# A two-layer encoder trunk: the first gate and up projections on unnormalised columns of x with the root of the norm applied later, and the matmuls of each bank sorted by width

## The chip, the cores and the metric

The kernel runs on one core of one Trainium2 chip. The metric is device time in microseconds (us) of one execution; the profile is one such execution on its own, and its times are read from the start of its span.

## The reference

Two layers, each a half-step SwiGLU feed-forward, a token mixing and a second half-step feed-forward. Every one of these six sub-layers normalises its input (root mean square, times a gain) and its output.

```
def rmsnorm(x, g):
    y = xf * lax.rsqrt(jnp.mean(xf * xf, axis=-1, keepdims=True) + NORM_EPS)
    return y * g
def swiglu(x, w_gate, w_up, w_down):
    return (jax.nn.silu(x @ w_gate) * (x @ w_up)) @ w_down
f = swiglu(rmsnorm(x, ffn1_pre_g[l]), ffn1_w_gate[l], ffn1_w_up[l], ffn1_w_down[l])
x = x + 0.5 * rmsnorm(f, ffn1_post_g[l])
```

x is 256 tokens by 1024 columns in float32, the gate and up weights are 1024 x 2816, the down weights 2816 x 1024. The root of the norm is one number per token, so it may be multiplied in before the projection, or after it on the projection's result. The token mixing (three groups of attention heads between one input and one output projection) is untouched by the change.

## The kernel before, in words

Precision is kept by splitting every float32 operand into a high part (rounded to the type that TensorE takes, fp32r) and the low remainder. A product then costs three products: high x high, high x low and low x high.

**Weights.** `Stream` takes all weights of both layers in one fixed list of chunks of 512 KB (for gate and up: 4 of the 8 rows of 128, times 256 columns). SP loads a chunk into one of 4 raw buffers (`load`, L116). `ahead(n)` cuts n half-chunks ("pieces"): ScalarE copies 128 x 512 into the high part `whi` (L139), VectorE subtracts to get the low part `wlo` (L140). After a chunk's second piece the next load is issued into the freed raw buffer. Nine chunks may be split ahead of the one in use (`NSPLIT`).

**Feed-forward, `ffn(i)`.** The activations lie in `xT`, columns on the partitions, 8 tiles, each with 256 tokens of high part beside 256 of low part. The first four of the 22 tiles of the hidden width (f = 0 to 3) go in token form (`gate`, `up`, `tokens_out`: tokens stationary, 256 weight columns moving, `mm3`, L373 to L375), one half of the tokens at a time, because the second half of the tokens is normalised later; their results are turned back by transposes (`token_close`, L507). The other 18 tiles (f = 4 to 20 in steps of two) go through `cols_pair`: two PSUM banks for gate and two for up per step. In a bank, for each of the 8 row tiles k, a wide matmul (128 x 512: high weights against high and low activations at once, L405) is followed by a narrow one (128 x 256: low weights against high activations, L407). After a bank ScalarE copies its low half out (L412), VectorE adds the halves (L413); after the second gate bank ScalarE takes silu (L552), after the second up bank VectorE multiplies (L558) and the product is split (L299, L300). Then `stream.ahead(6)` puts up to six pieces into the queues of ScalarE and VectorE. Four PSUM banks ("rot") turn in this loop. So VectorE's order in a step is fixed: two additions, pieces, two additions, product, split, pieces.

**Down, `down`.** 22 chunks of the down weights, 12 matmuls of 128 x 512 each, then post-norm, residual and the next pre-norm.

**The start.** x comes in rows (L185, L261), with the gain of the first norm broadcast to all partitions (L206) and the first four chunks behind it on SP's queue. `Norm.alone` squares x on ScalarE (L296), takes the root on GpSimd (L283), multiplies x by root and gain on VectorE (L345), TensorE transposes (L368) and ScalarE and VectorE split into `xT`. A hand-written list, `START`, places these steps between the pieces. 14 matmuls on `ident` keep TensorE at work before (L912). The gains of the next norms and the lambda vectors are loaded by GpSimd in the first feed-forward (L203, L198, L904).

Of the kernel before, what the change touches and what calls it, by code (L numbers as in the profile page):

```python
# [79 lines left out]


START = {
    "x1": 2,
    "warm": 14,
    "ops": [
        ["A0", "d", "p", "T00", "d", "T01", "p", "A1", "p"],
        ["d", "d"],
        ["d", "T10"],
        ["p", "T11"],
        ["d", "d", "d", "p", "d"],  # L90
    ],
}
WARM = START["warm"]
# [3 lines left out]
class Stream:  # L97
# [3 lines left out]
    def __init__(self, nc, raw_pool, split_pool):  # L101
        self.nc, self.raw_pool, self.split_pool = nc, raw_pool, split_pool
        self.src, self.raw, self.parts = [], {}, {}
        self.loaded = self.cut = self.used = self.piece = 0
        self.spare, self.in_spare = [], set()
# [4 lines left out]
    def load(self):  # L110
# [5 lines left out]
        self.nc.sync.dma_start(raw[:, : kt * n].rearrange("p (k n) -> p k n", n=n), ap)  # L116
        self.raw[i] = raw
        self.loaded += 1

    def ahead(self, pieces, lo=None):  # L120

        for _ in range(pieces):
            i = self.cut
            if i >= len(self.src):
                return
            if self.piece == 0:
                if i < self.used + NSPLIT + len(self.in_spare):
                    self.hi = self.split_pool.tile([P, CH], F32R, tag="whi", name=f"whi{i}")
# [10 lines left out]
            self.nc.scalar.copy(self.hi[:, a:b], raw[:, a:b])  # L139
            (lo or self.nc.vector).tensor_sub(self.lo[:, a:b], raw[:, a:b], self.hi.bitcast(F32)[:, a:b])  # L140
            self.piece += 1
            if self.piece == 2:
                self.parts[i] = (
                    self.hi[:, :m].rearrange("p (k n) -> p k n", n=n),
                    self.lo[:, :m].rearrange("p (k n) -> p k n", n=n),
                )
                self.raw.pop(i)
                self.cut, self.piece = i + 1, 0
                self.load()

    def get(self, i):
        return self.parts[i]
# [9 lines left out]
def trunk_kernel(  # L162
    ctx: ExitStack,
    tc: tile.TileContext,
    x, f1_pre, f1_gate, f1_up, f1_down, f1_post,
# [29 lines left out]
    def load_pre(i):  # L195
        if i < len(norms):
            pre_tiles[i] = work.tile([P, D], F32, tag="gpre", name=f"gpre{i}", bufs=1)
            nc.gpsimd.dma_start(pre_tiles[i], row_bcast(norms[i][0], norms[i][2], D))  # L198

    def load_post(i):  # L200
        if i < len(norms):
            post_tiles[i] = work.tile([P, D], F32, tag="gpost", name=f"gpost{i}", bufs=1)
            nc.gpsimd.dma_start(post_tiles[i], row_bcast(norms[i][1], norms[i][2], D))  # L203

    pre_tiles[0] = work.tile([P, D], F32, tag="gpre", name="gpre0", bufs=1)
    nc.sync.dma_start(pre_tiles[0], row_bcast(f1_pre, 0, D))  # L206
# [16 lines left out]
    def plan_ffn(gate, up, down, l):  # L223
        g = {}
        for key, ap, c0 in (("g", gate, 0), ("u", up, 0), ("g", gate, 1), ("u", up, 1)):
            for h in range(2):
                stream.add(rows(ap, l, 4 * h, 4 * h + 4, c0 * 256, c0 * 256 + 256), 4, 256)
        for f in range(4, KF, 2):
# [29 lines left out]

    for k in range(NRAW):
        if k == START["x1"]:  # L260
            nc.sync.dma_start(xs[:, 1, :], x_t[:, 1, :])  # L261
        stream.load()
# [5 lines left out]
    ones = work.tile([P, P], F32, tag="tc", bufs=3, name="ones")  # L268
# [33 lines left out]
    class Norm:  # L302
# [33 lines left out]
        def alone(self):  # L336

            t, nm = self.t, "pre" + self.nm
            ss = small.tile([P, 4], F32, tag="ss", name=f"sp_{nm}")
            self.xg = work.tile([P, D], F32, tag="xg", name=f"xg_{nm}", bufs=1)  # L340
            for h in range(2):
                mean_square(xs[:, t, HALVES[h]], ss, h, nm)
            r = rstd_of(halves_mean(ss, nm), 1, nm)
            for sl in HALVES:
                nc.vector.scalar_tensor_tensor(self.xg[:, sl], xs[:, t, sl], r[:, 0:1], pre_tiles[0][:, sl],  # L345
                                               ALU.mult, ALU.mult)

# [48 lines left out]
    def cols_pair(out, c, nm, between=lambda: None):  # L396

        for j in range(2):  # L400
            cs = slice(j * P, j * P + P)
            ps = psum.tile([P, 2, SEQ], F32, tag="rot", name=f"{nm}_{j}")
            for k in range(KT):
                wh, wl = stream.get(c + k // 4)
                nc.tensor.matmul(ps.rearrange("p a t -> p (a t)"), lhsT=wh[:, k % 4, cs],  # L405
                                 rhs=xT[:, k].rearrange("p a t c -> p (a t c)"), start=k == 0, stop=False)
                nc.tensor.matmul(ps[:, 1, :], lhsT=wl[:, k % 4, cs], rhs=xT[:, k, 0].rearrange("p t c -> p (t c)"),  # L407
                                 start=False, stop=k == KT - 1)
            if j == 0:
                between()  # L410
            side = work.tile([P, 512], F32, tag="tc", bufs=3, name=f"side_{nm}_{j}")[:, :SEQ]
            nc.scalar.copy(side, ps[:, 1, :])  # L412
            nc.vector.tensor_add(out[:, j, :], ps[:, 0, :], side)  # L413
# [53 lines left out]

    def ffn(i, turn1):
# [42 lines left out]
        sg00 = gate(0, 0, (lambda: start(1)) if i == 0 else None)  # L511
        if i == 0:
            start(2)
        h00 = up(sg00, 0, 0, (lambda: start(3)) if i == 0 else None)
        if i == 0:
            start(4)
        else:
            sg10 = gate(1, 0, turn1)
        sg01 = gate(0, 1)
        stream.done(2)  # L520
        if i == 0:
            stream.ahead(4)
        h01 = up(sg01, 0, 1)
        stream.done(2)
        stream.ahead(4)
        if i == 0:
            sg10 = gate(1, 0)
        sg11 = gate(1, 1)
        stream.done(2)
        stream.ahead(4)  # L530
        new_h()
        token_close(h00, 0, 0)
        h10 = up(sg10, 1, 0)
        token_close(h01, 0, 1)
        h11 = up(sg11, 1, 1)
        stream.done(2)
        stream.ahead(4)
        token_close(h10, 1, 0)
        load_pre(i + 1)
        if i % 3 == 0:  # L540
            load_lambda(i // 3)
        closing = [(h11, 1, 1)]
        for f in range(4, KF, 2):
            cc = stream.used

            def close():
                while closing:
                    token_close(*closing.pop())

            sg = work.tile([P, 512], F32, tag="ta", bufs=TA, name=f"sg{i}_{f}")  # L550
            cols_pair(sg.rearrange("p (a b) -> p a b", a=2), cc, f"pg{i}_{f}", close)
# [5 lines left out]
            cols_pair(hv, cc + 2, f"pu{i}_{f}")  # L557
# [3 lines left out]
            stream.ahead(6)  # L561
# [351 lines left out]
    first = [Norm(0, t) for t in range(2)]  # L913

    def start(n):
        for op in START["ops"][n]:
            if op == "d":
                stream.ahead(1)
            elif op == "p":
                stream.ahead(1, nc.gpsimd)  # L920
            elif op[0] == "A":
                first[int(op[1])].alone()
            else:
                first[int(op[1])].turn((int(op[2]),))

    start(0)
    load_post(0)
# [6 lines left out]
    "x", "ffn1_pre_g", "ffn1_w_gate", "ffn1_w_up", "ffn1_w_down", "ffn1_post_g",  # L934
# [32 lines left out]
```

## Time and profile before

| | us |
|---|---|
| three runs | 1020.24, 1024.27, 1023.5; median 1023.5 |
| the profiled execution, device time | 1022.65 |
| its span in the profile | 1020.7 |
| TensorE busy in the span | 996.7 (98%) |
| VectorE / ScalarE busy | 672.3 / 586.4 |
| first useful matmul | 11.59 |
| first wide matmul of the first feed-forward | 43.48 |
| first matmul of its down stage | 146.84 |

Between the device time and the span lie 1.95 us that no row shows. Instructions are pipelined, so the time of one row is longer than the step from its start to the next one's start; the steps are what adds up.

### The profile page before, as it was taken

How to read it: one execution, taken by the hardware profiler on the slowest of the kernel's cores; microseconds unless marked ns; L12 is line 12 of the kernel's file. 1: busy time of each engine (PE TensorE's matmuls, PEld its weight loads, DVE VectorE, ACT ScalarE, POOL GpSimd, SP SyncE). 2: the span in 40 equal slices, each digit the busy share in tenths (PEclk: the TensorE clock that was granted, in tenths of full speed). 3: DMA queues.
4: the chain of work that ended last, by engine and by line, in shares of the span. 5: the costliest groups of instructions: out<-in, count | busy, mean ns of one | idle time of the engine just before them, and what ended most of it. 6: DMA issues, size and time to landing. Idle time of an engine off the chain costs nothing.

```text
span 1020.7 us, 16031 instructions
## 1 busy us (share of the span) xinstructions
PE 996.7 (98%) x5940; PEld 874.6 (86%) x5940; DVE 672.3 (66%) x1345; ACT 586.4 (57%) x1265; POOL 43.2 (4%) x73
## 2 busy tenths in 40 slices
PE   8899999999999999999999999999989999999997
PEld 7788888899887988888899888888978789888886
DVE  4576675577686577765557767646678756866642
ACT  5465564466766566555446756545577655765531
POOL 3100000010000100000020000001000010000000
PEclk8999999999999999999999999999999999999999
DMA  8866656748344477656726865663853525765631
GB/s 265 234 201 181 196 171 228 199 131 235 101 145 124 145 219 217 185 201 210 223 69 206 249 197 173 227 192 118 253 150 105 158 90 175 240 202 189 215 114 41
DMA packets 151005, 183.16 MB, mean 179 GB/s; under 512 B 5744, under 2 KB 134896, under 8 KB 150928
## 3 DMA queue, kind: packets, MB, share of 16 engines
q1 hardware_dynamic: 148448, 174.08, 55.7%
q0 software_dynamic: 2192, 7.54, 2.5%
q8 instruction: 46, 0.75, 0.3%
q10 hardware_dynamic: 288, 0.52, 0.1%
q14 instruction: 31, 0.25, 0.1%
HBM read 181.08 MB, written 1.05 MB: 178 GB/s over the span
## 4 chain that ended last, share of the span: by engine, by line
PE 83%; DVE 5%; DMA 5%; ACT 4%; issue 1%; POOL 0%; SPq 0%; DVEq 0%; POOLq 0%; ACTq 0%
PE pg L405 13%; PE pu L405 13%; PE acc L373 9%; PE acc L375 9%; PE acc L374 9%; PE pg L407 7%; PE pu L407 7%; DVE wlo L140 3%; DMA raw<-in_w_in_dram 2%; PE pp L373 2%; DMA raw<-in_ffn_w_up_dram 2%; PE pp L375 2%; PE pp L374 1%; ACT p_b L722 1%; PE pu L374 1%
## 5 line engine op out<-in xcount | busy, mean ns | idle before, releaser
L140 DVE TENSOR_TENSOR wlo<-raw,whi 128x512 fp32r<-128x512 f32 (+1 forms) x625 | 395.6, 688 | 157.1 <-ACT whi L139 156.8
L139 ACT CAST whi<-raw 128x512 fp32r<-128x512 f32 x630 | 349.8, 617 | 122.0 <-PE acc L375 71.3
L405 PE MATMUL pg<-xT,whi 128*128 128x512 f32 x576 | 207.1, 401 | 0.0
L405 PE MATMUL pu<-xT,whi 128*128 128x512 f32 x576 | 205.2, 399 | 0.0
L407 PE MATMUL pg<-xT,wlo 128*128 128x256 f32 x576 | 162.3, 282 | 0.0
L407 PE MATMUL pu<-xT,wlo 128*128 128x256 f32 x576 | 161.8, 281 | 0.0
L373 PE MATMUL acc<-whi,hh 128*128 128x512 f32 x352 | 137.2, 390 | 0.0
L374 PE MATMUL acc<-wlo,hh 128*128 128x512 f32 x352 | 137.0, 389 | 0.0
L375 PE MATMUL acc<-whi,hl 128*128 128x512 f32 x352 | 137.0, 389 | 0.0
L405 PEld LDWEIGHTS pg<-xT,whi 128*128 128x128 f32 x576 | 108.9, 189 | 26.7
L405 PEld LDWEIGHTS pu<-xT,whi 128*128 128x128 f32 x576 | 108.2, 188 | 27.0
L407 PEld LDWEIGHTS pg<-xT,wlo 128*128 128x128 f32 x576 | 109.5, 190 | 0.0
L407 PEld LDWEIGHTS pu<-xT,wlo 128*128 128x128 f32 x576 | 108.8, 189 | 0.0
L375 PEld LDWEIGHTS acc<-whi,hl 128*128 128x128 f32 x352 | 66.1, 188 | 13.9
L373 PEld LDWEIGHTS acc<-whi,hh 128*128 128x128 f32 x352 | 66.1, 188 | 13.6
L374 PEld LDWEIGHTS acc<-wlo,hh 128*128 128x128 f32 x352 | 66.1, 188 | 13.4
L373 PE MATMUL pp<-xT,whi 128*128 128x256 f32 x256 | 76.4, 298 | 0.0
L374 PE MATMUL pp<-xT,whi 128*128 128x256 f32 x256 | 73.0, 285 | 0.0
L375 PE MATMUL pp<-xT,wlo 128*128 128x256 f32 x256 | 73.0, 285 | 0.0
L412 ACT COPY side_pu<-pu 128x256 f32<-128x256 f32 x72 | 26.1, 368 | 50.3 <-PE pu L407 50.3
L373 PEld LDWEIGHTS pp<-xT,whi 128*128 128x128 f32 x256 | 49.4, 193 | 4.9 <-issue 4.2
L413 DVE TENSOR_TENSOR h<-pu,side_pu 128x256 f32<-128x256 f32 x72 | 29.8, 422 | 30.4 <-ACT side_pu L412 30.2
(247 smaller groups left out, 1455.1 us busy)
## 6 DMA issues: line engine op xcount, KB each, us to landing
raw<-in_ffn_w_gate_dram SPq DMA_DIRECT2D x88, 512.0 KB, 4.8
raw<-in_ffn_w_up_dram SPq DMA_DIRECT2D x88, 512.0 KB, 4.6
raw<-in_ffn_w_down_dram SPq DMA_DIRECT2D x88, 512.0 KB, 4.4
raw<-in_w_in_dram SPq DMA_DIRECT2D x36, 512.0 KB, 5.3
raw<-in_w_out_dram SPq DMA_DIRECT2D x16, 512.0 KB, 3.5
raw<-in_w_in_dram SPq DMA_DIRECT2D x8, 576.0 KB, 4.3
gpost<-in_ffn_post_g_dram POOLq DMA_DIRECT2D x4, 512.0 KB, 4.3
raw<-in_w_in_dram SPq DMA_DIRECT2D x4, 384.0 KB, 3.4
```

The lines of the kernel that those rows point to most:

```text
L139: self.nc.scalar.copy(self.hi[:, a:b], raw[:, a:b])
L140: (lo or self.nc.vector).tensor_sub(self.lo[:, a:b], raw[:, a:b], self.hi.bitcast(F32)[:, a:b])
L373: nc.tensor.matmul(ps, lhsT=ah, rhs=bh, start=first, stop=False)
L374: nc.tensor.matmul(ps, lhsT=ah, rhs=bl, start=False, stop=False)
L375: nc.tensor.matmul(ps, lhsT=al, rhs=bh, start=False, stop=last)
L405: nc.tensor.matmul(ps.rearrange("p a t -> p (a t)"), lhsT=wh[:, k % 4, cs], rhs=xT[:, k].rearrange("p a t c -> p (a t c)"), start=k == 0, ...
L407: nc.tensor.matmul(ps[:, 1, :], lhsT=wl[:, k % 4, cs], rhs=xT[:, k, 0].rearrange("p t c -> p (t c)"), start=False, stop=k == KT - 1)
L412: nc.scalar.copy(side, ps[:, 1, :])
L413: nc.vector.tensor_add(out[:, j, :], ps[:, 0, :], side)
L722: nc.scalar.activation(p[:, a:b], p[:, a:b], AF.Exp, bias=st[:, t : t + 1], scale=-1.0, accum_out=st[:, 2 + t : 3 + t])
```

## The change

**The start.** The host lays x out a second time, in columns (`x_cols`, with the first gain as 8 columns ahead of it; a transposition, no arithmetic). SP loads it in four quarters of 256 KB, each followed by half a gate chunk. `prepare` multiplies columns by the gain while it splits them (ScalarE's copy with a scale, VectorE's multiply-subtract); the root is left out. f = 0 to 3 now go in column form too (`cols_pieces`: for each quarter of x, 6 narrow matmuls into each of two banks), for all 256 tokens at once, with no transposes. Squares are taken on ScalarE and summed on GpSimd while the first up projection runs; a matmul with ones sums over partitions, GpSimd takes the root, and a second matmul with a diagonal spreads it into `rb` (128 x 256). VectorE multiplies every gate and up result of the first feed-forward by `rb`: per bank for f = 0 to 3, per pair of banks (128 x 512) in the nine steps of the loop. `START` is gone, and so are the transposes of x; 10 matmuls on `ident` stand ahead instead of 14. The rows of x, needed for the residual, are loaded at f = 10 and f = 16, the first post gain, the second pre gain and the lambda vectors after f = 20, the gains on SP's queue instead of GpSimd's. `ahead` takes 4 pieces instead of 6 up to f = 4 of the first feed-forward.

**All four feed-forwards.** `cols_pair` issues the eight wide matmuls of a bank first and the eight narrow ones behind them. The first four tiles of the other three feed-forwards stay in token form.

```
+    def pass_hi(ps, c, k, cs):
+        wh = stream.get(c + k // 4, k % 4 // 2)[0]
+        nc.tensor.matmul(ps.rearrange("p a t -> p (a t)"), lhsT=wh[:, k % 4, cs],
+                         rhs=xT[:, k].rearrange("p a t c -> p (a t c)"), start=k == 0, stop=False)
...
             for k in range(KT):
-                wh, wl = stream.get(c + k // 4)
-                nc.tensor.matmul(ps.rearrange("p a t -> p (a t)"), lhsT=wh[:, k % 4, cs],
-                                 rhs=xT[:, k].rearrange("p a t c -> p (a t c)"), start=k == 0, stop=False)
-                nc.tensor.matmul(ps[:, 1, :], lhsT=wl[:, k % 4, cs], rhs=xT[:, k, 0].rearrange("p t c -> p (t c)"),
-                                 start=False, stop=k == KT - 1)
+                pass_hi(ps, c, k, cs)
+            for k in range(KT):
+                pass_lo(ps, c, k, cs)
...
+        def prepare(p):
+            for k in (2 * p, 2 * p + 1):
+                hi, lo = (xT[:, k, b].rearrange("p t c -> p (t c)") for b in range(2))
+                nc.scalar.activation(hi, xc[:, k, :], AF.Copy, scale=gcol[:, k : k + 1])
+                nc.vector.scalar_tensor_tensor(lo, xc[:, k, :], gcol[:, k : k + 1], hi.bitcast(F32),
+                                               ALU.mult, ALU.subtract)
+            stream.ahead(1)
+        def before_up(p):
+            for n in ((0, 1), (2,), (3,), ())[p]:
+                squares(n)
+            stream.ahead(1)
...
+        pg = cols_pieces(c, "pg0_0", prepare, lambda p: None, "acc")
+        pu = cols_pieces(c + 2, "pu0_0", before_up, after_up)
...
+                cols_pair(sv, cc, f"pg{i}_{f}", close)
+                if rb is not None:
+                    nc.vector.tensor_mul(sv, sv, rb.unsqueeze(1).broadcast_to([P, 2, SEQ]))
             nc.scalar.activation(sg, sg, AF.Silu)
             stream.done(2)
-            stream.ahead(6)
+            stream.ahead(4 if rb is not None and f < 6 else 6)
...
+            if i == 0 and f in (10, 16):
+                t = int(f == 16)
+                nc.sync.dma_start(xs[:, t, :], x_t[:, t, :])
+            if i == 0 and f == KF - 2:
+                load_post(0, nc.sync)
+                load_pre(1, nc.sync)
+                load_lambda(0)
```

How instructions stand on the engines, at three places. TensorE at the first banks of the loop, before; `pg0_4_0` is gate bank 0 of f = 4, `whi8` and `wlo8` the parts of its first chunk, `pth` a transpose of the token form:

```order
L405 MATMUL pg0_4_0_547<-xT_83,whi8_328 128x512
L407 MATMUL pg0_4_0_547<-xT_83,wlo8_329 128x256
...
L405 MATMUL pg0_4_0_547<-xT_83,whi9_363 128x512
L407 MATMUL pg0_4_0_547<-xT_83,wlo9_364 128x256
...
L507 MATMUL pth0_1_1_564<-ident_84,ht0_1_1_515 128x128 x2
L405 MATMUL pg0_4_1_572<-xT_83,whi8_328 128x512
L407 MATMUL pg0_4_1_572<-xT_83,wlo8_329 128x256
```

The same banks now (L389 is the wide matmul, L394 the narrow one):

```order
L389 MATMUL pg0_4_0_490<-xT_81,whi8_401 128x512 x4
L389 MATMUL pg0_4_0_490<-xT_81,whi9_409 128x512 x4
L394 MATMUL pg0_4_0_490<-xT_81,wlo8_402 128x256 x4
L394 MATMUL pg0_4_0_490<-xT_81,wlo9_410 128x256 x4
L389 MATMUL pg0_4_1_510<-xT_81,whi8_401 128x512 x4
L389 MATMUL pg0_4_1_510<-xT_81,whi9_409 128x512 x4
L394 MATMUL pg0_4_1_510<-xT_81,wlo8_402 128x256 x4
L394 MATMUL pg0_4_1_510<-xT_81,wlo9_410 128x256 x4
```

Where wide and narrow took turns, eight of a kind now stand together, and the transposes are gone. SP's queue at the start, before:

```order
L185 DMA xs_78<-in_x_dram 128x512 x2
L206 DMA gpre0_81<-in_ffn1_pre_g_dram 128x1024
L116 DMA raw0_91<-in_ffn1_w_gate_dram 128x4x256
L116 DMA raw1_93<-in_ffn1_w_gate_dram 128x4x256
L261 DMA xs_78<-in_x_dram 128x1024
L116 DMA raw2_96<-in_ffn1_w_up_dram 128x4x256
L116 DMA raw3_98<-in_ffn1_w_up_dram 128x4x256
```

And now, with `came` for the columns of x:

```order
L263 DMA came_80<-in_x_cols_dram 128x520
L111 DMA raw0_89<-in_ffn1_w_gate_dram 128x2x256
L263 DMA came_80<-in_x_cols_dram 128x512
L111 DMA raw0_89<-in_ffn1_w_gate_dram 128x2x256
L263 DMA came_80<-in_x_cols_dram 128x512
L111 DMA raw1_94<-in_ffn1_w_gate_dram 128x2x256
L263 DMA came_80<-in_x_cols_dram 128x512
L111 DMA raw1_94<-in_ffn1_w_gate_dram 128x2x256
L106 DMA raw2_99<-in_ffn1_w_up_dram 128x4x256
```

The broadcast gain is out of the queue's head, and x and gate weights come in turns. VectorE in step f = 8 of the first feed-forward, before:

```order
L413 TENSOR_TENSOR sg0_8_803<-pg0_8_0_804,side_pg0_8_0_821 128x256
L413 TENSOR_TENSOR sg0_8_803<-pg0_8_1_824,side_pg0_8_1_841 128x256
L140 TENSOR_TENSOR wlo25_846<-raw25_733,whi25_845 128x512 x2
L140 TENSOR_TENSOR wlo26_854<-raw26_741,whi26_853 128x512 x2
L413 TENSOR_TENSOR h0_8_861<-pu0_8_0_862,side_pu0_8_0_879 128x256
L413 TENSOR_TENSOR h0_8_861<-pu0_8_1_882,side_pu0_8_1_899 128x256
L558 TENSOR_TENSOR h0_8_861<-sg0_8_803,h0_8_861 128x512
L300 TENSOR_TENSOR hl1_0_451<-h0_8_861,hh1_0_449 128x512
```

And at f = 6 now:

```order
L400 TENSOR_TENSOR sg0_6_609<-pg0_6_1_630,side_pg0_6_1_647 128x256
L645 TENSOR_TENSOR sg0_6_609<-sg0_6_609,rb_129 128x512
L135 TENSOR_TENSOR wlo16_653<-raw16_538,whi16_652 128x512 x2
L135 TENSOR_TENSOR wlo17_661<-raw17_546,whi17_660 128x512 x2
L135 TENSOR_TENSOR wlo18_669<-raw18_599,whi18_668 128x512 x2
L400 TENSOR_TENSOR h0_6_676<-pu0_6_0_677,side_pu0_6_0_694 128x256
L400 TENSOR_TENSOR h0_6_676<-pu0_6_1_697,side_pu0_6_1_714 128x256
L657 TENSOR_TENSOR h0_6_676<-h0_6_676,rb_129 128x512
L658 TENSOR_TENSOR h0_6_676<-sg0_6_609,h0_6_676 128x512
L303 TENSOR_TENSOR hl1_0_382<-h0_6_676,hh1_0_380 128x512
```

Two multiplications by `rb` (L645, L657) stand in each step, ahead of silu and ahead of the product; a step asks for three chunks per half until nine are ahead.

More of the change, by code (lines that the diff above doesn't have):

```diff
@@ L78 @@
 NSPLIT = 9
[L82 to L93, printed above, removed]
+WARM = 10
 TA = 4
@@ L102, in __init__ @@
         self.nc, self.raw_pool, self.split_pool = nc, raw_pool, split_pool
-        self.src, self.raw, self.parts = [], {}, {}
+        self.src, self.raw, self.parts, self.ready = [], {}, {}, {}
         self.loaded = self.cut = self.used = self.piece = 0
@@ L108, in add, with load @@
         self.src.append((ap, kt, n))
-    def load(self):
+    def load(self, before=None):
         i = self.loaded
@@ L115, in load @@
         raw = self.raw_pool.tile([P, CH], F32, tag="raw", name=f"raw{i}")
-        self.nc.sync.dma_start(raw[:, : kt * n].rearrange("p (k n) -> p k n", n=n), ap)
+        rv = raw[:, : kt * n].rearrange("p (k n) -> p k n", n=n)
+        if before is None:
+            self.nc.sync.dma_start(rv, ap)
+        else:
+            for h in range(2):
+                before(h)
+                ks = slice(h * kt // 2, (h + 1) * kt // 2)
+                self.nc.sync.dma_start(rv[:, ks], ap[:, ks])
         self.raw[i] = raw
@@ L141, in ahead @@
             self.piece += 1
+            self.parts[i] = (
+                self.hi[:, :m].rearrange("p (k n) -> p k n", n=n),
+                self.lo[:, :m].rearrange("p (k n) -> p k n", n=n),
+            )
+            self.ready[i] = self.piece
             if self.piece == 2:
[L143 to L146, printed above, removed]
                 self.raw.pop(i)
@@ L183, in trunk_kernel @@
     x_t = x.rearrange("b (t p) d -> (b p) t d", p=P)
-    for h in range(2):
-        nc.sync.dma_start(xs[:, 0, h * 512 : h * 512 + 512], x_t[:, 0, h * 512 : h * 512 + 512])
+    first = act.tile([P, 1536], F32, tag="bigh2", name="first")
+    ones, diag = first[:, :P], first[:, P : 3 * P]
     def row_bcast(ap2d, row, n):
@@ L223, in plan_ffn @@
     def plan_ffn(gate, up, down, l):
[L224 to L228, printed above, removed]
+        if stream.src:
+            for ap, c0 in ((gate, 0), (up, 0), (gate, 256), (up, 256)):
+                for h in range(2):
+                    stream.add(rows(ap, l, 4 * h, 4 * h + 4, c0, c0 + 256), 4, 256)
+            f0 = 4
+        else:
+            f0 = 0
+        for f in range(f0, KF, 2):
             for ap in (gate, up):
@@ L409, in cols_pair, with cols_pieces @@
             if j == 0:
                 between()
-            side = work.tile([P, 512], F32, tag="tc", bufs=3, name=f"side_{nm}_{j}")[:, :SEQ]
-            nc.scalar.copy(side, ps[:, 1, :])
-            nc.vector.tensor_add(out[:, j, :], ps[:, 0, :], side)
+            taken(out[:, j, :], ps, f"{nm}_{j}")
+    def cols_pieces(c, nm, before, after, tag="rot"):
+        pss = [psum.tile([P, SEQ], F32, tag=tag, name=f"{nm}_{j}") for j in range(2)]
+        for p in range(4):
+            before(p)
+            for j in range(2):
+                for k in (2 * p, 2 * p + 1):
+                    wh, wl = (w[:, k % 4, j * P : j * P + P] for w in stream.get(c + k // 4, k % 4 // 2))
+                    mm3(pss[j], wh, wl, xT[:, k, 0], xT[:, k, 1], k == 0, k == KT - 1)
+            after(p)
+        return pss
@@ L509, in token_close, with close @@
             split_copy(hT_hi(2 * p, 2)[:, :, ts], hT_lo(2 * p, 2)[:, :, ts], pt)
-        sg00 = gate(0, 0, (lambda: start(1)) if i == 0 else None)
+        def close():
+            while closing:
+                token_close(*closing.pop())
+        closing = []
+        rb = None
         if i == 0:
[L513 to L516, printed above, removed]
-        else:
+            rb, before, after = first_columns(c, lambda: (new_h(), hT_hi(0, 2), hT_lo(0, 2))[1:])
+            f0 = 2
+        else:
+            sg00 = gate(0, 0)
+            h00 = up(sg00, 0, 0)
@@ L518, in ffn @@
             sg10 = gate(1, 0, turn1)
-        sg01 = gate(0, 1)
-        stream.done(2)
-        if i == 0:
+            sg01 = gate(0, 1)
+            stream.done(2)
+            h01 = up(sg01, 0, 1)
+            stream.done(2)
             stream.ahead(4)
[L523 to L543, printed above, removed]
+            sg11 = gate(1, 1)
+            stream.done(2)
+            stream.ahead(4)
+            new_h()
+            token_close(h00, 0, 0)
+            h10 = up(sg10, 1, 0)
@@ L544, in ffn @@
+            token_close(h01, 0, 1)
+            h11 = up(sg11, 1, 1)
+            stream.done(2)
+            stream.ahead(4)
+            token_close(h10, 1, 0)
+            closing = [(h11, 1, 1)]
+            f0 = 4
+            load_pre(i + 1)
+            if i % 3 == 0:
+                load_lambda(i // 3)
+        for f in range(f0, KF, 2):
             cc = stream.used
-            def close():
-                while closing:
-                    token_close(*closing.pop())
+            early = i == 0 and f == 2
@@ L560, in ffn @@
             stream.done(2)
-            stream.ahead(6)
+            stream.ahead(4 if rb is not None and f < 6 else 6)
+            if i == 0 and f in (10, 16):
[5 more added lines that the diff above has]
+                load_lambda(0)
         def free():
@@ L912, in trunk_kernel @@
         nc.tensor.matmul(warm[:, :P], lhsT=ident, rhs=ident, start=True, stop=True)
[L913 to L927, printed above, removed]
     turn1 = None
```

115 lines of the change are left out of this document (87 added, 28 removed).

## The prediction

> **What bounds the kernel now.** I read the page first: who is busy, where it is not full, and who carries the chain that ended last.
>
> ```profile
> span 1020.7 us, 16031 instructions
> PE 996.7 (98%) x5940; PEld 874.6 (86%) x5940; DVE 672.3 (66%) x1345; ACT 586.4 (57%) x1265; POOL 43.2 (4%) x73
> PE   8899999999999999999999999999989999999997
> PE 83%; DVE 5%; DMA 5%; ACT 4%; issue 1%; POOL 0%; SPq 0%; DVEq 0%; POOLq 0%; ACTq 0%
> L405 PE MATMUL pg<-xT,whi 128*128 128x512 f32 x576 | 207.1, 401 | 0.0
> L405 PE MATMUL pu<-xT,whi 128*128 128x512 f32 x576 | 205.2, 399 | 0.0
> ```
>
> TensorE carries the kernel. Time can be won only where it stands still, which is the first 50 us, or by shorter steps between its matmuls. The last two rows count what the change sorts: 1152 wide matmuls, eight to a bank, so 144 banks, 36 in each of the four feed-forwards. Next the timeline of the start (start, duration, idle time before in brackets):
>
> ```profile
> 1.42 5.27 PE L912 MATMUL warm<-ident 128*128 128x128 f32 x28 [1.42 <-POOL ident masks.py:199]
> 3.49 0.63 ACT L296 ACTIVATE junk_pre<-xs 128x512 bf16<-128x512 f32 x1 [1.41 <-DMA xs<-in_x_dram]
> 4.24 0.63 ACT L296 ACTIVATE junk_pre<-xs 128x512 bf16<-128x512 f32 x1
> 8.55 1.41 DVE L345 SCALAR_TENSOR_TENSOR xg_pre<-xs,r_pre,gpre 128x512 f32<-128x512 f32 x2 [3.34 <-DMA gpre<-in_ffn_pre_g_dram]
> 11.59 0.58 PE L373 MATMUL pg<-whi,xT 128*128 128x256 f32 x1 [0.26 <-ACT xT L299]
> 33.13 0.28 PE L373 MATMUL pu<-whi,xT 128*128 128x256 f32 x1
> ...
> 35.53 0.28 PE L375 MATMUL pu<-whi,xT 128*128 128x256 f32 x1
> ...
> 38.62 0.28 PE L375 MATMUL pu<-whi,xT 128*128 128x256 f32 x1
> 43.14 0.69 PE L507 MATMUL pth<-ident,ht 128*128 128x128 f32 x2 [4.24 <-DVE ht L501]
> 43.48 0.78 PE L405 MATMUL pg<-xT,whi 128*128 128x512 f32 x1
> ...
> 46.62 0.39 PE L405 MATMUL pg<-xT,whi 128*128 128x512 f32 x1
> ```
>
> Three losses stand here: no useful matmul before 11.59, because VectorE waits for the broadcast gain; 4.24 us of idle before 43.14; and the five pairs from 43.48 to 46.62, which take 3.14 us where five take 1.76 later (8 pairs in 2.82, below): 1.4 us at the half clock after the idle time.
>
> **The change part by part.** *Wide first.* The steps, from the timeline of TensorE in the loop (first and ninth wide matmul) and in a down stage (first and last of 25 in a row):
>
> ```profile
> 119.99 0.40 PE L405 MATMUL pu<-xT,whi 128*128 128x512 f32 x1
> 120.22 0.28 PE L407 MATMUL pu<-xT,wlo 128*128 128x256 f32 x1
> 120.33 0.40 PE L405 MATMUL pu<-xT,whi 128*128 128x512 f32 x1
> ...
> 122.81 0.40 PE L405 MATMUL pu<-xT,whi 128*128 128x512 f32 x1
> 199.68 0.39 PE L375 MATMUL acc<-whi,hl 128*128 128x512 f32 x1
> ...
> 205.12 0.39 PE L375 MATMUL acc<-whi,hl 128*128 128x512 f32 x1
> ```
>
> A bank of eight turns costs 122.81 - 119.99 = 2.82 us, 0.3525 a pair. Wide behind wide steps by 5.44 / 24 = 0.2267; narrow behind narrow (33.13 to 35.53 above, 20 steps) by 0.120. A sorted bank has seven of each and one mixed pair: 7 x 0.2267 + 7 x 0.120 + 0.3525 = 2.78. So 0.0405 us is saved a bank: 36 x 0.0405 = 1.5 us in each feed-forward, 5.8 in 144 banks. Nothing hides it, since TensorE is the bound. A sorted bank asks for its last high piece after 1.6 us instead of 2.5 and for the low pieces later; once chunks lie ahead that costs nothing. What makes a turn dearer than its two parts no row shows; the rows of sorted matmuls come from other stages, which is the risk.
>
> [...]
>
> *The start.* The first 256 KB came at 3.49, and 512 KB were there by 4.24 (ScalarE reads the second half then without a wait). Now these are a quarter of x and half a gate chunk. What ScalarE, VectorE and GpSimd need for the splitting, the products and the sums (groups of the page and of the list by shape, and one row of the timeline):
>
> ```profile
> L139 ACT CAST whi<-raw 128x512 fp32r<-128x512 f32 x618 | 343.0, 617 | 113.0 <-PE acc L375 62.2 <-DMA raw<-in_w_in_dram 14.8 <-issue 12.8
> L140 DVE TENSOR_TENSOR wlo<-raw,whi 128x512 fp32r<-128x512 f32 x613 | 387.8, 688 | 149.3 <-ACT whi L139 149.0
> L558 DVE TENSOR_TENSOR h<-sg,h 128x512 f32<-128x512 f32 x36 | 24.9, 693 | 1.2
> L668 DVE TENSOR_TENSOR z_c<-s_c,negmask 128x256 f32<-128x256 f32 x12 | 5.0, 418 | 0.5 <-PE s_c L665 0.5
> 11.12 1.28 POOL L140 TENSOR_TENSOR wlo<-raw,whi 128x512 fp32r<-128x512 f32 x1 [5.28 <-ACT whi L139]
> GB/s 0 105 339 137 148 337 347 410 383 354 303 279 232 311 264 211 186 330 311 280 343 245 273 211 253 143 31 184 218 256 377 378 242 110 300 180 279 160 317 343
> ```
>
> From 4.24: high part 0.62, low part 0.69, so 5.6; the matmuls on `ident` end at 1.42 + 5.27 x 10/14 = 5.2. First group whole at 5.7. The last row is DMA in slices of 1.25 us: 137 and 148 fall where the broadcast gain is read, 340 and more around it. Without it a quarter of x with half a gate chunk (524 KB) takes 1.54 us, so the fourth is there at 4.24 + 4.6 = 8.9, split at 10.2, and its 12 matmuls (1.44) end at 11.7. Since TensorE waits between groups I add one loss of clock, 1.4: gate done at 13.1. By 140 GB/s throughout it would be 5 us later, my upper bound. A rule bears on the 1.4: the Trainium skill ("TensorE: Matmul & The Clock Gate", What's actually happening) lets the clock fall after a whole idle window of about 3.4 us. The trace's 4.24 us of idle agrees; waits under 1 us would cost nothing, and the sum by that rule is 1.4 lower.
>
> The other 144 narrow matmuls of f = 0 to 3 take 17.3: 30.4. The sum over partitions and the spread of the root add some 0.5 on TensorE (four narrow steps). Three waits follow from the queues. VectorE takes the mean for the root behind the up projection, and the low part of the next chunk stands behind it: 0.2 + 0.69 = 0.9. The next two chunks' pieces stand behind the first products by `rb` (0.4). The first high part of f = 4 stands on ScalarE behind the silu of f = 2, and that behind six operations of VectorE (four for `h` of f = 0, two for the gate of f = 2, together 0.42 x 4 + 0.69 x 2 = 3.1, plus 0.6 for the split between) that follow the pieces of chunk 7: some 1.0 more than the 5.8 of the up projection hides. Together 2.3; bounds 0 (the queues keep up) and 4. GpSimd's seven additions of 128 x 256 (half the 1.28 of the row, 4.5 in all, from about 11) are done before the up projection ends at 19. Loop begins: 30.4 + 0.5 + 2.3 = 33.2 against 43.48. The 16 and 8 transposes of before lie inside that difference.
>
> *Multiplying by `rb`.* `rb` is read with a broadcast; L668 reads one too and costs what a plain 128x256 does, so two multiplications a step at 0.69, ahead of silu and product. What VectorE has to spare, from its timeline and ScalarE's in one step:
>
> ```profile
> 107.93 0.42 DVE L413 TENSOR_TENSOR sg<-pg,side_pg 128x256 f32<-128x256 f32 x1 [0.39 <-ACT side_pg L412]
> 109.56 2.50 DVE L140 TENSOR_TENSOR wlo<-raw,whi 128x512 fp32r<-128x512 f32 x4 [1.21 <-ACT whi L139]
> 113.58 0.43 DVE L413 TENSOR_TENSOR h<-pu,side_pu 128x256 f32<-128x256 f32 x1 [1.18 <-ACT side_pu L412]
> 115.42 0.69 DVE L300 TENSOR_TENSOR hl<-h,hh 128x512 fp32r<-128x512 f32 x1 [0.69 <-ACT hh L299]
> 119.23 0.42 DVE L413 TENSOR_TENSOR sg<-pg,side_pg 128x256 f32<-128x256 f32 x1 [0.38 <-ACT side_pg L412]
> 113.17 0.37 ACT L412 COPY side_pu<-pu 128x256 f32<-128x256 f32 x1 [1.82 <-PE pu L407]
> ```
>
> In 11.30 us it waits for TensorE's bank 0.39 + 1.18 = 1.57; the waits of 1.21 and 0.69 are for silu and split, part of the chain. Two multiplications with their hand-over take 1.45, and TensorE's step gets 4 x 0.0405 = 0.16 shorter: 1.57 - 1.45 - 0.16 = -0.04. The chain just breaks even. But while the lead grows from two chunks to nine, the code asks for 12 pieces a step, not 8: 4 x 0.60 ((2.50 - 0.69) / 3 a piece) = 2.4 us a step, some three steps, 7 us. The four banks let TensorE run three ahead, 8.3 us, of which the slow start has used part. Following both queues with these durations, TensorE waits 2.7 in all around f = 10 to 14; bounds 0 (lag fits the banks) and 8 (piece and product a tenth dearer, 0.6 a step on the chain).
>
> *The loads moved to f = 10, 16 and after f = 20.* Two gains on SP's queue ahead of down chunks: 1.05 MB at the 140 GB/s above is 7.5 us. Nine chunks are split ahead, each good for 12 x 0.2267 = 2.72 us, 24 us of cover: nothing. Without the cover 7.5.
>
> *Sum.* Down begins at 33.2 + 36 x 2.78 + 2.7 = 136.0, not
>
> ```profile
> 146.84 0.40 PE L373 MATMUL acc<-whi,hh 128*128 128x512 f32 x1
> ```
>
> so 10.8 less, and 108 x 0.0405 = 4.4 less in the other three: 15.2. The profiled execution took 1022.65 (span and 1.95 around it): 1007.5. The median of the runs is 0.85 higher: 1008.
>
> **The rivals.** *Order is neutral* (the dearer turn has to do with these operands, not with the turn): 5.8 back, 1014. Against it: both pure steps are measured; for it: the wide one not with weights stationary. [...]
>
> *VectorE holds the first loop*: waits of 8 or more instead of 2.7, down from 141, 1014. For it: a margin of -0.04. With both, 1020.
>
> *A run of wide matmuls into one bank costs more here* (slower). There are 7 x 144 = 1008 wide-behind-wide steps, so each ns is 1 us. From 15 ns (0.242) the whole gain is gone; from 20 ns (0.247) it is slower by over 0.5%; at 0.255, 1036. The turn's own wide step, 119.99 to 120.22, is 0.23, and the down stage's run into one bank 0.227, both against it.
>
> **How the numbers follow.** About 0.5%, 5 us, is what a measurement can tell from no change. Forecast 0.63: own range 1002 (no lag, no clock loss, no waits: 6.4 less) to 1013 (slow DMA); of it 0.25 goes to a clock that never falls, by itself 1006.6. Neutral order 0.12, VectorE 0.13, both 0.04 (within 0.5%), dearer runs 0.05, something unnamed that cancels the gain 0.03. Faster 0.63 + 0.12 + 0.13 = 0.88; the same 0.07; slower 0.05. 1002 to 1016 leaves out the last three cases.
>
> **What would show it.** Right: first useful matmul near 5.7, first wide one near 33, first down matmul near 136, wide steps of 0.227 and narrow of 0.120 in every bank. Wrong: TensorE waiting for `wlo` or for a bank through most of the first loop, a half clock lasting past 20 us, a bank of 2.82, or waits in the first down stage.

## The result and the profile after

| | before | after |
|---|---|---|
| median of the runs, us | 1021.87 (4 runs, 1020.15 to 1024.27) | 1006.79 (4 runs, 1005.79 to 1008.49) |
| profiled execution: device time / span, us | 1022.65 / 1020.7 | 1006.07 / 1004.4 |

The ratio is 0.9852 with a 95% interval of [0.9823, 0.9882]: 15.1 us faster, where the prediction said 1008.0 and 1002 to 1016. The order's term was mis-sized, the start came out near the forecast by other terms, and one gain stood in no term.

The page of the changed kernel, the lines that answer to those of before:

```profile
span 1004.4 us, 16001 instructions
PE 984.4 (98%) x5914; PEld 867.6 (86%) x5914; DVE 686.6 (68%) x1373; ACT 584.2 (58%) x1262; POOL 41.8 (4%) x72
PE   8999999998999999999999999999989999999997
PE 80%; DVE 9%; ACT 6%; DMA 3%; issue 2%; POOL 0%; SPq 0%; POOLq 0%; DVEq 0%; ACTq 0%
L389 PE MATMUL pg<-xT,whi 128*128 128x512 f32 x576 | 145.2, 394 | 1.6 <-DVE sg L400 0.9
```

TensorE still carries the kernel. VectorE's share of the chain rose from 5% to 9%, and for the first time the wide matmuls wait for it (last column of the last row). TensorE's timeline at the start of the changed kernel (start, duration, idle time before in brackets):

```profile
1.42 4.64 PE L1020 MATMUL warm<-ident 128*128 128x128 f32 x20 [1.42 <-POOL ident masks.py:199]
5.71 0.56 PE L364 MATMUL pg<-xT,whi 128*128 128x256 f32 x1
...
6.79 0.31 PE L365 MATMUL pg<-xT,whi 128*128 128x256 f32 x1
...
7.65 0.28 PE L366 MATMUL pg<-xT,wlo 128*128 128x256 f32 x1
8.16 0.39 PE L364 MATMUL pg<-xT,whi 128*128 128x256 f32 x1 [0.23 <-ACT whi L134]
...
8.88 0.39 PE L366 MATMUL pg<-xT,wlo 128*128 128x256 f32 x1 [0.22 <-DVE wlo L135]
...
13.05 0.28 PE L364 MATMUL pu<-xT,whi 128*128 128x256 f32 x1
...
13.64 0.38 PE L366 MATMUL pu<-xT,wlo 128*128 128x256 f32 x1 [0.19 <-DVE wlo L135]
...
20.62 0.39 PE L366 MATMUL pg<-xT,wlo 128*128 128x256 f32 x1 [0.52 <-DVE wlo L135]
...
33.52 2.30 PE L389 MATMUL pg<-xT,whi 128*128 128x512 f32 x8 [0.63 <-ACT whi L134]
136.57 0.40 PE L364 MATMUL acc<-whi,hh 128*128 128x512 f32 x1
```

The first useful matmul starts at 5.71 instead of 11.59, the first wide one at 33.52 instead of 43.48, the down stage at 136.57 instead of 146.84. Where the 16.4 us between the two spans lie (1020.75 and 1004.37), by the start of each stage's first matmul:

| stage | before | after | gained |
|---|---|---|---|
| start, to the first wide matmul | 43.5 | 33.5 | 10.0 |
| loop of the first feed-forward | 103.4 | 103.1 | 0.3 |
| the three other loops | 102.02, 102.01, 102.01 | 100.84, 100.83, 100.84 | 3.5 |
| projection stage of the two mixings | 70.5 and 70.7 | 69.3 and 69.2 | 2.7 |
| all the rest | | | -0.1 |

The 2.7 us in the mixing, whose code is the same, came as a surprise. The windows of TensorE there (window, its length, busy time and matmuls, granted clock, DMA share, GB/s), before:

```profile
250.00:262.00 12.00, 9.74 (x73) 0.86 0.36 114
747.00:760.00 13.00, 10.16 (x76) 0.87 0.42 117
```

and the same windows of the changed kernel:

```profile
250.00:262.00 12.00, 12.00 (x103) 1.00 0.45 134
747.00:760.00 13.00, 13.00 (x108) 1.00 0.38 119
```

Each mixing of before holds one stretch of 3.4 us at the half clock (a clock of 0.86 over 12 us), the changed kernel none. The experiments show below that these stretches come and go with the old start and the new one, with either order.

### The profile page after: what moved, and what is told of

It reads as the page before. It is cut to its first block, busy times and chain, and to the rows that moved or that the text cites. A ratio compares the mean times of both kernels' runs of the same rounds, so it can differ in the third digit from the quotient of the medians.

```text
span 1004.4 us, 16001 instructions
## 1 busy us (share of the span) xinstructions
PE 984.4 (98%) x5914; PEld 867.6 (86%) x5914; DVE 686.6 (68%) x1373; ACT 584.2 (58%) x1262; POOL 41.8 (4%) x72
## 3 DMA queue, kind: packets, MB, share of 16 engines
HBM read 181.60 MB, written 1.05 MB: 182 GB/s over the span
## 4 chain that ended last, share of the span: by engine, by line
PE 80%; DVE 9%; ACT 6%; DMA 3%; issue 2%; POOL 0%; SPq 0%; POOLq 0%; DVEq 0%; ACTq 0%
PE pu L389 12%; PE pg L389 11%; PE acc L364 9%; PE acc L366 9%; PE acc L365 9%; PE pu L394 6%; PE pg L394 6%; DVE wlo L135 5%; DMA raw<-in_w_in_dram 2%; PE pp L364 2%; PE pp L366 1%; PE pp L365 1%; ACT whi L134 1%; PE pu L366 1%; PE pu L365 1%
## 5 line engine op out<-in xcount | busy, mean ns | idle before, releaser
L135 DVE TENSOR_TENSOR wlo<-raw,whi 128x512 fp32r<-128x512 f32 x630 | 399.5, 688 | 146.2 <-ACT whi L134 145.8
L389 PE MATMUL pg<-xT,whi 128*128 128x512 f32 x576 | 145.2, 394 | 1.6 <-DVE sg L400 0.9
L389 PE MATMUL pu<-xT,whi 128*128 128x512 f32 x576 | 144.4, 392 | 0.4 <-DVE h L400 0.4
L389 PEld LDWEIGHTS pg<-xT,whi 128*128 128x128 f32 x576 | 103.3, 189 | 21.1 <-ACT whi L134 1.5
L389 PEld LDWEIGHTS pu<-xT,whi 128*128 128x128 f32 x576 | 103.6, 189 | 19.2 <-DVE h L400 0.6
L394 PEld LDWEIGHTS pg<-xT,wlo 128*128 128x128 f32 x576 | 78.6, 190 | 5.6
L394 PEld LDWEIGHTS pu<-xT,wlo 128*128 128x128 f32 x576 | 78.6, 190 | 5.6
L394 PE MATMUL pg<-xT,wlo 128*128 128x256 f32 x576 | 80.3, 282 | 0.0
L394 PE MATMUL pu<-xT,wlo 128*128 128x256 f32 x576 | 80.3, 282 | 0.0
L302 ACT CAST hh<-h 128x512 fp32r<-128x512 f32 x38 | 23.6, 621 | 64.4 <-DVE h L658 62.0
L364 PEld LDWEIGHTS pp<-xT,whi 128*128 128x128 f32 x256 | 48.8, 191 | 4.7 <-issue 4.0
L365 PEld LDWEIGHTS pp<-xT,whi 128*128 128x128 f32 x256 | 48.9, 191 | 0.0
```

Of the source, the lines that this page charges most:

```text
L302: nc.scalar.copy(hi, src)
L364: nc.tensor.matmul(ps, lhsT=ah, rhs=bh, start=first, stop=False)
L365: nc.tensor.matmul(ps, lhsT=ah, rhs=bl, start=False, stop=False)
```

## The experiments

Three theories stood at the start. *A*: sorting is worth some 1.2 us a loop, because a change between wide and narrow matmuls is dear; the start is worth 10; two multiplications by `rb` a step are a little too much for VectorE, and 2.2 us are lost there. *B*: order is neutral, and what the loops gained comes from somewhere else. *C*: the gain of the start comes from the broadcast gain that left the queue, not from columns.

**e1: the new start, matmuls in turns.** In the changed kernel, `cols_pair` issues wide and narrow in turns again.

```
             for k in range(KT):
                 pass_hi(ps, c, k, cs)
-            for k in range(KT):
                 pass_lo(ps, c, k, cs)
```

> The changed kernel with the order in a bank undone (wide and narrow in turns again), the new start kept. Theory (start and order add up): the first wide matmul stays near 33.5 us, the loops of the three other feed-forwards go from 100.8 back to 102.0 us each, in all some 4 us over the changed kernel, near 1011. Rival (order does nothing, the shorter loops come with the start or the clock): loops stay at 100.8, time near 1007.

Measured: 1009.63 (5 runs), 0.9896 [0.9873, 0.9919]; here and below this is the ratio to the kernel before, run anew beside the experiment, with its 95% interval. The three later loops took 102.0 each, as before the change, so what they gained is the order's. In the first loop it was otherwise: 102.6, half a microsecond *less* than sorted. Two pieces of its timeline, eight turns apart each, in the first loop and in the second:

```profile
119.72 0.39 PE L389 MATMUL pu<-xT,whi 128*128 128x512 f32 x1
...
122.49 0.39 PE L389 MATMUL pu<-xT,whi 128*128 128x512 f32 x1
...
379.63 0.40 PE L389 MATMUL pg<-xT,whi 128*128 128x512 f32 x1
...
382.45 0.40 PE L389 MATMUL pg<-xT,whi 128*128 128x512 f32 x1
```

Eight turns take 2.77 us in the first loop and 2.82 in the second: 347 ns a turn and 353. In the second loop one turn in three takes 360 or 361 ns and the others 349 or 350; in the first nearly all take 343 to 350. With the new start a turn in the first loop costs no more than its parts (227 + 120 = 347), and sorting gains nothing there. The mixings held their half-clock stretches in this kernel,

```profile
240.00:250.00 10.00, 8.23 (x55) 0.83 0.34 109
735.00:747.00 12.00, 8.72 (x69) 0.91 0.30 100
```

and took 70.4 and 70.8, so 2.7 of the 5.3 us by which its span (1009.7) is longer are theirs and not the order's.

**e2: sorted matmuls alone.** The kernel before, with the second half of the loop body in a loop of its own.

```
                 nc.tensor.matmul(ps.rearrange("p a t -> p (a t)"), lhsT=wh[:, k % 4, cs], ...)
+            for k in range(KT):
+                wh, wl = stream.get(c + k // 4)
                 nc.tensor.matmul(ps[:, 1, :], lhsT=wl[:, k % 4, cs], ...)
```

> The kernel before with the sorted order alone, the old start kept. Theory: the three other loops go from 102.0 to 100.8, the first from 103.3 to about 102, in all 4 to 5 us less than before, near 1017.5; the query-key stretch of the mixings takes 69.3 or 70.7 us as its clock happens to fall, whatever the start. Rival (order does nothing): 1022. Second rival (the new start is what keeps the clock up in the mixings): they stay at 70.5 here.

Measured: 1017.29 (12 runs), 0.9967 [0.995, 0.9985]. The later loops took 100.8 each, as in the changed kernel: theory B falls, the order by itself gains 1.2 us a loop. The first loop took 103.1 because half-clock time reaches further into it here (from 42.3 to 49.1 us; before, from 42.9 to 46.3). The first mixing took 68.7, without a half-clock stretch, the second 70.3 with one, on the code of before. e1 kept both stretches with the new start. So they do not come with the change; whether one kernel has them in one execution and not in the next no trace shows.

**e3: no `rb` in the loop.** The changed kernel without its two multiplications; the root is left out for f = 4 to 20.

```
-                if rb is not None:
-                    nc.vector.tensor_mul(sv, sv, rb.unsqueeze(1).broadcast_to([P, 2, SEQ]))
...
-                if rb is not None:
-                    nc.vector.tensor_mul(hv, hv, rb.unsqueeze(1).broadcast_to([P, 2, SEQ]))
```

> The changed kernel without the two multiplications by rb in each of the nine steps of the first loop (the root is left out of the results of f = 4 to 21). Theory (VectorE's chain makes the waits of the first loop): the loop goes from 103.1 to about 101.4 us, the waits for the additions of L400 go, 0.6 us for the pieces of f = 4 stays. Rival (the thin lead of chunks at its begin makes them): 103 stays.

Measured: 1004.71 (4 runs), 0.9841 [0.9812, 0.9869], and the first loop took 100.8, like the others. Waits of TensorE from 30 to 140 us (in total, times, longest) in the changed kernel:

```profile
PE pg L389 <- DVE sg L400: 0.9, 1, 0.9
PE pg L389 <- ACT whi L134: 0.6, 1, 0.6
PE pu L389 <- DVE h L400: 0.4, 1, 0.4
```

and without the multiplications:

```profile
PE pg L389 <- ACT whi L134: 0.6, 1, 0.6
```

Both waits for VectorE go, and the 2.2 us with them: the first steps before and behind a wait are slower too, so that 1.3 of waiting make some 2.2 of delay. The multiplications cause them.

**e4: runs of 16.** Both banks of a projection take their wide matmuls first, then both their narrow ones, so that the width changes half as often.

```
...
-            for k in range(KT):
-                pass_hi(ps, c, k, cs)
-            for k in range(KT):
-                pass_lo(ps, c, k, cs)
+        for j in range(2):
+            for k in range(KT):
+                pass_hi(pss[j], c, k, cuts[j])
+        between()
+        for j in range(2):
+            for k in range(KT):
+                pass_lo(pss[j], c, k, cuts[j])
+            taken(out[:, j, :], pss[j], f"{nm}_{j}")
```

> The changed kernel with runs twice as long: 16 wide matmuls into both banks of a pair, then 16 narrow ones. Theory (the first five wide steps behind a narrow one are dearer, 27 ns in all, 8 of which the narrow ones give back): the dear steps come once a pair, not once a bank, loops 100.8 to 100.45, in all 1.4 us less. Rival (the dear steps belong to the row tile k): they show twice in 16, loops stay at 100.8.

Measured: 1005.43 (4 runs), 0.9851 [0.9827, 0.9874]; the loops took 102.7 and three times 100.5. The median steps by place in a run tell what a sorted bank pays. After a change of width the wide steps take 233, 236, 228, 232 and 231 ns and then 227; with runs of 16 the same five are dear, and the ten behind them take 227. So the surplus of some 20 ns is paid once a run. Half as many runs gained 0.3 us a loop: 18 x 0.02 = 0.36.

**e5: the root on GpSimd.** VectorE keeps the gate's multiplication; the up result's is done on GpSimd, on the silu.

```
             nc.scalar.activation(sg, sg, AF.Silu)
+            if rb is not None and not early:
+                nc.gpsimd.tensor_mul(sv, sv, rb.unsqueeze(1).broadcast_to([P, 2, SEQ]))
...
-                if rb is not None:
-                    nc.vector.tensor_mul(hv, hv, rb.unsqueeze(1).broadcast_to([P, 2, SEQ]))
```

> The changed kernel with the second multiplication by rb of each step moved: GpSimd multiplies silu's result by rb while the up banks run, VectorE's multiplication of the up result goes. Theory (the multiplications cost 2.3 us of waits because they stand in VectorE's chain): with half of them gone the first loop takes 101 to 101.8 us instead of 103.1, in all 1 to 2 us less than the changed kernel. Rival (GpSimd's 128x512, about 1.3 us by its row before, slows VectorE or comes late for the product): the loop stays at 103 or grows.

Measured: 1007.19 (4 runs), 0.9878 [0.986, 0.9895]; the first loop took 103.3, nothing won. The timelines of GpSimd and VectorE around one step, in the next step VectorE's subtractions alone, and the durations of the subtraction (least, median, most):

```profile
67.53 1.30 POOL L648 TENSOR_TENSOR sg<-sg,rb 128x512 f32<-128x512 f32 x1 [12.14 <-ACT sg L646]
68.00 4.39 DVE L135 TENSOR_TENSOR wlo<-raw,whi 128x512 fp32r<-128x512 f32 x6 [1.21 <-ACT whi L134]
81.43 4.39 DVE L135 TENSOR_TENSOR wlo<-raw,whi 128x512 fp32r<-128x512 f32 x6 [1.21 <-ACT whi L134]
L135 DVE TENSOR_TENSOR wlo<-raw,whi x630: 551/684/1387, 5.5 to 974.3; 128x512 fp32r<-128x512 f32 x154, 128x576 fp32r<-128x576 f32 x2, 128x384 fp32r<-128x384 f32 x2
```

The same subtractions of both steps in the changed kernel, where VectorE multiplies itself and GpSimd rests:

```profile
68.18 3.90 DVE L135 TENSOR_TENSOR wlo<-raw,whi 128x512 fp32r<-128x512 f32 x6 [1.21 <-ACT whi L134]
81.78 3.70 DVE L135 TENSOR_TENSOR wlo<-raw,whi 128x512 fp32r<-128x512 f32 x6 [1.21 <-ACT whi L134]
```

While GpSimd multiplies for 1.30 us, the first subtraction that VectorE begins takes about 1376 ns instead of 684, in each of the nine steps. VectorE is spared a multiplication of 0.69 a step, and its six subtractions take 0.5 longer in the first of these two steps and 0.7 in the second.

**e6: the gain ahead again.** The changed kernel with the broadcast gain (512 KB written, 128 copies of one row) at the head of SP's queue.

```
+    pre_tiles[0] = work.tile([P, D], F32, tag="gpre", name="gpre0", bufs=1)
+    nc.sync.dma_start(pre_tiles[0], row_bcast(f1_pre, 0, D))
```

> The changed kernel with the broadcast of the first gain read again at the head of SP's queue (nobody uses it). Theory (the broadcast reads at 140 GB/s and the columns of x stand behind it): the first useful matmul and the first wide one come 3.5 to 4.5 us later, near 9.5 and 37.5. Rival (it costs its bytes at 340 GB/s): 1.5 us later.

Measured: 1009.77 (4 runs), 0.9903 [0.9888, 0.9918]; first wide matmul at 36.2, 2.7 later. The timeline of TensorE shows that only a part of this is transfer:

```profile
1.42 4.64 PE L1022 MATMUL warm<-ident 128*128 128x128 f32 x20 [1.42 <-POOL ident masks.py:199]
7.44 0.58 PE L366 MATMUL pg<-xT,whi 128*128 128x256 f32 x1 [1.38 <-ACT whi L134]
...
13.45 0.39 PE L368 MATMUL pg<-xT,wlo 128*128 128x256 f32 x1
13.67 0.29 PE L366 MATMUL pg<-xT,whi 128*128 128x256 f32 x1
13.79 0.28 PE L367 MATMUL pg<-xT,whi 128*128 128x256 f32 x1
```

The first matmul starts 1.7 us later. But now TensorE stands idle for 1.38 us ahead of it, and every step from there to 13.45 takes about 0.21 instead of 0.12: the clock has not risen. In the changed kernel the matmuls on `ident` run into the first useful one, and the steps fall to 0.12 at 6.8. So 27 steps lose some 0.09 each, 2.5 us. The clock's first rise, as the trace records it, comes at 13.7 here, and between 4.7 and 7.6 in the other eleven traces. Of the changed kernel's own delays (below) 0.6 of half clock and 1.0 of waits fall away in return: 1.7 + 2.5 - 1.6 = 2.6. The 3.5 to 4.5 us expected for a broadcast at 140 GB/s did not come: the first matmul's 1.7 is nearer to the rival's 1.5, and from 2.5 us on no slice of 1.25 us is below 257 GB/s here.

**e7: e4 and e5 together.**

> Runs of 16 and the root on GpSimd together. If they add up: first loop near 101.2, the others 100.5, some 2.5 to 3 us under the changed kernel, near 1004. Rival (longer runs hold banks longer, so VectorE's lag shows again): no better than either alone, 1005.4.

Measured: 1006.07 (4 runs), 0.987 [0.9852, 0.9888]; loops of 103.3 and 100.5. In the three later loops the runs of 16 win their 0.3 each, as in e4. In the first loop nothing is won, not even the 0.3 that e4 had there, so the expected sum did not come.

**e8: the old start without the gain.** The kernel before with the gain's load replaced; the first gain is left out of the result.

```
-    nc.sync.dma_start(pre_tiles[0], row_bcast(f1_pre, 0, D))
+    nc.vector.memset(pre_tiles[0], 1.0)
```

> The kernel before with its first gain not read but set to one by VectorE (the first norm's gain is left out); all else as it was. Theory (the broadcast at the queue's head costs some 3.5 us, and root, transposes and the token form cost the rest of the 10): the first useful matmul comes near 8.5 instead of 11.6, the first wide one 2 to 4 us earlier than 43.5. Rival (the loads of weights set the time of the first wide matmul whatever comes before): it stays at 43.

Measured: 1016.86 (10 runs), 0.9977 [0.9955, 0.9999]. First useful matmul at 8.85, first wide one at 40.55, 2.9 earlier than before the change. Its waits of TensorE in the first 50 us:

```profile
PE pth L507 <- DVE ht L501: 3.2, 1, 3.2
PE pt L368 <- DVE xg_pre L345: 1.9, 1, 1.9
```

The wait of 3.2 at the end of the token form stays, as do the transposes. By e6 and e8 the gain's place in the queue is worth 2.7 to 2.9 of the 10.0 us, in e6 as much through the clock as through the transfer. The other 7 belong to the rest of the new start (columns, no transposes, the order of the loads), which no run takes apart. Theory C falls. This kernel's first loop, with turns, again ran at 347 ns a turn, and took 101.7 although it began at the half clock.

**e9: no root on the up results.** The second normalisation divides each token of the feed-forward's result by its own root mean square, so a factor per token on the up results falls out again, up to the 1e-6 that is added under that root. The changed kernel with `rb` on the gate alone:

```
-                nc.vector.tensor_mul(hv, hv, rb.unsqueeze(1).broadcast_to([P, 2, SEQ]))
```

and likewise for f = 0 to 3, where the product with the gate takes the place of the product with `rb`.

> The changed kernel with the root left out of the up results of the first feed-forward altogether. A factor per token on its output is taken out again by the norm behind it, up to the 1e-6 that the norm adds to the mean square. Nothing takes the place of VectorE's nine multiplications (and of four small ones at the start). Theory (VectorE's time in the chain makes the waits, wherever it goes): first loop 103.1 to about 101.4 us, in all near 1005. Rival (the waits come from one multiplication as much as from two, as on GpSimd): 103 stays.

Measured: 1004.75 (5 runs), 0.9845 [0.9823, 0.9866]. TensorE's window over most of the first loop:

```profile
50.00:150.00 100.00, 100.00 (x553) 1.00 0.75 240
```

No wait is left, and the loop took 100.8. One multiplication a step fits into VectorE's time, two do not. The first wide matmul came at 32.47, 1.05 earlier: the wait of 0.63 ahead of it is gone, as the first products are fewer too. The rest is not explained; in e10, with the same start, it came at 33.12.

**e10: e9 with runs of 16.**

> The same with runs of 16. If both add up: first loop near 101.1, the other three 100.5, near 1003.5 to 1004. Rival (longer runs hold the banks longer and bring the lag back): first loop 102 or more, 1005.

Measured: 1003.02 (5 runs, 1001.91 to 1004.31), 0.9829 [0.9805, 0.9852], the fastest of all; the loops took 100.5 each, all four. Its interval overlaps that of the changed kernel, so the difference rests on the stages: the loops are 2.52 and 3 x 0.34 shorter, the start 0.40, and 2.17 were given back in the mixings, which held half-clock stretches in its profile (70.3 each). That makes 1.8, the difference of the spans (1002.6 and 1004.4).

## Why the prediction was right

**Wide first: right in kind, a fifth too high.** The prediction summed seven pure steps of each kind and one mixed pair to 2.78 us a bank. A bank of the second feed-forward in the changed kernel:

```profile
380.09 2.00 PE L389 MATMUL pg<-xT,whi 128*128 128x512 f32 x8
381.94 1.12 PE L394 MATMUL pg<-xT,wlo 128*128 128x256 f32 x8
382.89 1.32 PE L389 MATMUL pu<-xT,whi 128*128 128x512 f32 x5
```

It takes 382.89 - 380.09 = 2.80. Eight wide steps take 1.85 and not 8 x 0.2267 = 1.81: the term that failed is "wide behind wide steps by 0.2267", taken from a run of 25 in the down stage, while in a run of eight the five dear first steps are most of it (e4). By the means over the later loops, turns cost 8 x 353.2 ns = 2.826 us a bank and sorted ones 7 x 230.5 + 226.7 + 7 x 118.9 + 120 = 2.792. So 34 ns are saved a bank and not 40.5: 36 x 0.034 = 1.2 us a loop, and the three later ones gained 3.5 where 4.4 was forecast. In the first loop the same 1.2 is saved against the turns of before; but e1 shows that it isn't the order's: with the new start the turns would have cost 347, 2.77 a bank, a little less than sorted. The rival *neutral order* holds, then, for one loop of four. So a step is not the same whatever stands beside it: the same turn took 353 or 347 ns, and the same wide step 227 to 236.

**Start: 33.2 forecast, 33.5 measured, by other terms.** First group at 5.7: right. Gate done at 13.1: 13.05, but neither by the fourth quarter's arrival nor by a lost clock after the waits, so that the two agree is luck. 48 steps of 0.12 make 5.8, the first steps at the half clock (5.71 to 6.79, and to 7.65 for twelve) add 0.6, and two waits with the slow steps behind them add 1.0. The waits come from ScalarE, whose timeline in the changed kernel is

```profile
6.68 0.91 ACT L495 ACTIVATE xT<-came 128x256 fp32r<-128x256 f32 x2 [1.26 <-DMA came<-in_x_cols_dram]
7.50 0.60 ACT L134 CAST whi<-raw 128x512 fp32r<-128x512 f32 x1
8.13 0.91 ACT L495 ACTIVATE xT<-came 128x256 fp32r<-128x256 f32 x2
8.94 0.60 ACT L134 CAST whi<-raw 128x512 fp32r<-128x512 f32 x1
9.55 0.91 ACT L495 ACTIVATE xT<-came 128x256 fp32r<-128x256 f32 x2
```

Behind its first pieces it waits for x once, until 6.68; from there a group takes it 8.13 - 6.68 = 1.45, just what TensorE needs for 12 steps, and TensorE waits no more in the gate projection. The 1.4 for "one loss of clock" was not paid there: no wait was longer than 0.3, and the steps came back to 0.12. The clock rule cited beside that term (the Trainium skill, "TensorE: Matmul & The Clock Gate", What's actually happening) agrees in this. But the clock fell after less idle time than the whole window that this rule asks for: before the change the granted clock went to 0.50 at 8.8, when TensorE had stood still for 2.1 us, and in the mixings it fell behind stretches of 1.8; the traces decide here. e6 adds the rule's other half, since the same section lets the clock rise only after a whole busy window of about 3.4 us: an idle stretch of 1.38 ahead of the rise cost 27 slow steps. Of the three waits behind the gate projection, 2.3 in the sum, two came as described: 0.52 at 20.62 for the low part behind the mean, forecast 0.9, and 0.63 at 33.52 for the first high part of f = 4, forecast 1.0. Small ones such as that at 13.64, with the slow steps behind each, make up the rest. One loss of before stood on no list: the half clock that began at 8.8 held the first useful matmuls too, 17 steps from 11.59 to 15.66 that take 4.07 us where 17 x 0.12 is 2.0. The new start pays 0.6 for the half clock in its place.

**`rb`: right.** A margin of -0.04 us a step and waits of 2.7 in the first loop were forecast; 2.2 were lost, at

```profile
79.58 2.14 PE L389 MATMUL pg<-xT,whi 128*128 128x512 f32 x8 [0.91 <-DVE sg L400]
85.88 2.14 PE L389 MATMUL pu<-xT,whi 128*128 128x512 f32 x8 [0.43 <-DVE h L400]
```

which is f = 12, in the stretch named (f = 10 to 14). The margin was the right thing to look at: with one multiplication less it is 0.7 (half of 1.45 more) and nothing waits (e9). e3 and e9 show the cause by taking it away. The rival *VectorE holds the first loop* needed 8 us.

**Moved loads: nothing, right.** The first down stage took 60.8 in both kernels.

**What no term held.** Two half-clock stretches in the mixings, 2.7 us of the profiled difference. Such stretches stand in 15 of the 24 mixings of the twelve traces, each behind an idle stretch of 1.8 to 1.9 us that all 24 hold. Without TensorE's waits, the stage takes 65.7 us where there is none and 67.0 to 67.2 where there is one, so each costs 1.4 to 1.5; the waits differ by up to 2 us more, so that e6's first mixing took 70.2 without one. e1, e3, e4, e9 and e10 kept both with the new start; e2 and e8 lost one with the old one. So the 15.2 of the sum became 16.4 thus: 0.5 less by the start of the down stage (10.3 for 10.8), 0.9 less in the later loops, 2.7 more in the mixings, which the change did not cause and which are luck, and 0.1 less in the rest.

## What to carry to other kernels

A step's cost is read from a run of the length that the new order will have: the first five steps after a change of width were dearer, so a price from a run of 25 did not hold for a run of eight. Where work is moved to an engine with some slack, its margin a step (here -0.04 us) is worked out with the hand-over counted; halving the added work was worth more than moving it to an engine that blocks the first. And the matmuls that keep TensorE's clock up at the start have to reach the first useful one without a gap.

## What the runs showed of the hardware

- A 128 x 512 multiplication on GpSimd (1.30 us) held up a VectorE subtraction of two operands in on-chip memory from 684 to about 1376 ns each time (e5). The Trainium skill ("SBUF — State Buffer", SBUF: two separate sides) says so for a VectorE instruction with two inputs there against a GpSimd one that reads there: the one that starts first keeps the shared pair of ports for its whole instruction. The trace agrees: the subtraction that began 0.47 us after the multiplication ended 0.55 after its end.
- An idle stretch of 1.38 us before the clock had risen kept TensorE's steps at 0.21 for another 6 us (e6), while the profile's row of the granted clock says 1.00 there: up to the first rise the steps tell the clock, not that row.
- After a change from narrow to wide, the next five wide steps took 233, 236, 228, 232 and 231 ns, then 227; why five is open.
- The same turn of a wide and a narrow matmul cost 347 ns in the first loop of e1 and e8 and 353 in all their later loops and in all four of before, where one turn in three takes 360 or 361 and the others 349 or 350. What differs there was not found.
- Stretches of 3.4 us at the half clock in the mixings cost 1.4 to 1.5 us each and came and went between kernels with the same code there, behind idle stretches of 1.8 us; why one idle stretch brings the clock down and the next does not is open.
